# The down projection of a decoder layer: running sums in PSUM banks, weight differences on VectorE, chunks of eight pairs

## The chip, the cores and the metric

The kernel runs on one core of a Trainium2 chip. A core has a matrix engine (TensorE, in the profile PE; PEld is its weight load), VectorE (DVE), ScalarE (ACT), GpSimd (POOL) and SyncE (SP), which issues most of the DMAs. TensorE's products land in eight banks of PSUM, everything else works in SBUF. The metric is the device time of one execution in microseconds; before the change three runs took 1473.42, 1476.03 and 1476.26 us, a median of 1476.03 us.

## The reference

One decoder layer over 1024 tokens of width 1024. The part that the change touches is the second half of the MLP with its residual, and the final norm, in float32:

```
def squared_relu_mlp(xn, w_ff1, w_ff2):
    hdn = jnp.square(jax.nn.relu(xn @ w_ff1))      # [1024, 4096]
    return hdn @ w_ff2                             # the down projection, [1024, 1024]

h = h + mixer_block(...)
h = h + squared_relu_mlp(rmsnorm(h, norm_mlp_gain[l]), w_ff1[l], w_ff2[l])
return rmsnorm(h, norm_final_gain)
```

## The kernel before, in words

The large products are made in 2 x 2 blocks with seven block products instead of eight (Strassen's algorithm in Winograd's form). For the down projection the blocks are halves of the tokens (rows), of a pair of hidden tiles (contraction) and of the width (columns). With `b11`, `b12`, `b21`, `b22` the blocks of a weight pair, and `a11`, `a12`, `a22` and the sums `s1` to `s4` the hidden side, which the up projection has left in DRAM (`hid_d`), the products are P1 = a11 b11, P2 = a12 b21, P3 = s4 b22, P4 = a22 T4, P5 = s1 T1, P6 = s2 T2 and P7 = s3 T3, with T1 = b12 - b11, T2 = b22 - T1, T3 = b22 - b12 and T4 = b21 - T2. With U2 = P1 + P6 and U3 = U2 + P7, the blocks of the result are P1 + P2, U2 + P5 + P3, U3 + P4 and U3 + P5, each on top of the residual (`h2_d`).

Float32 accuracy is reached by splitting: `split_unit` makes of a [128, 512] operand a high part (ScalarE, L110, `da` and `db` on the hidden and on the weight side) and a low part (VectorE, L111: operand minus high part). Each product of two operands is three matmuls: high-high, high-low, low-high. A unit (one pair of hidden tiles in one of the seven products) takes 12 matmuls: three for each of four token tiles, which sit in four PSUM banks.

Before, the 16 pairs of hidden tiles go in four chunks of `NQ` = 4. A chunk runs its seven products one after the other, four units each: 28 products of 48 matmuls, 1344 in all. The units are split four ahead of their use (`wpool` has five buffers for each of its two tags). After each product `collect` empties its four banks into a sum of its own in SBUF (`accp...`, eight places of four tiles; four of them begin as the residual): VectorE adds (L267), or in the first chunk ScalarE copies (L1236). The banks are then free for another product, which begins afresh. The weight differences T1 to T4 are made by GpSimd (`sums`, L1205), into `temps` (`down_temp`) or in place. In the last chunk, whose order is P1, P2, P5, P6, P3, P7, P4, the sums over the products are made as well: GpSimd's `late_sums` after P6 (twelve additions, L267 on POOL), additions on VectorE, and the final norm of each row of tokens: `row_share` (a square sum on ScalarE, L1216, and a multiplication by the gain on GpSimd, L1218) and `row_end` (square sum L1222, square root L1223, reciprocal L1225, two scalings L1226 and L1227, and the stores).

What sets the order: the program is traced in the order of the code, and a scheduler puts each engine's instructions into a fixed list; each engine and the SyncE queue then work through their lists in order, waiting on semaphores. SBUF for the large operands is eight slots of 2 MB (`slot`), which the weights (`y...`), the hidden operands (`x...`) and the sums (`accp...`) take as they come free. `first_loads` starts the loads while the last group of the up projection runs, and all of them are issued by SyncE.

Of the kernel before, what the change touches and what calls it, by code (L numbers as in the profile page):

```python
# [22 lines left out]
NT = SEQ // P          # token tiles  # L23
KT = D // P            # contraction tiles over the model width
# [4 lines left out]
NM = DFF // P          # hidden tiles  # L29
LATE = 6               # token tiles from here on get the second norm's factors on ScalarE  # L30
EARLY = 4              # pairs of hidden tiles whose first products fill the gap of the second norm
NQ = 4                 # pairs of hidden tiles per chunk of the down projection
NORM_EPS = 1e-6        # of the group norm too
NEG_INF = -1e30

# tiles of 128 x 1024 in the weight stream
# [51 lines left out]
def block_kernel(ctx, tc, x, xT, wbig, cols, rows, ctab, amask, amask_u, out):  # L88
# [28 lines left out]
    def gmm(ps, lhsT, rhs, start, stop):  # L117
        """A large product; pieces of the background follow it."""
        pe.matmul(ps, lhsT=lhsT, rhs=rhs, start=start, stop=stop)  # L119
        bg.tick(ps.shape[-1] / 2.4)  # L120

# [46 lines left out]
    causal = const.tile([P, P], F32, name="causal")      # [key, query]: key <= query  # L168
# [32 lines left out]
    units = [0]  # L201

    def split_unit(name, src):
        """A [128, 512] operand in its two parts."""
# [5 lines left out]
    def w_raw(bl, g):  # L210
        """b11, b21, b12, b22 of a pair of tiles with the weights stationary."""
# [38 lines left out]
    def four(slot_, i):  # L250
        """Half i of a slot: four tiles of [128, 512]."""
# [941 lines left out]
    with tc.tile_pool(name="p6", bufs=1) as p6:  # L1193
# [37 lines left out]
        def collect(c, n, banks, tts):  # L1231
            """The banks of a product into its sum; in the last chunk also the sums over the products."""
            for tt in tts:
# [8 lines left out]
                if c < nchunk - 1:  # L1242
                    continue
# [158 lines left out]
```

## Time and profile before

| | |
|---|---|
| median of three runs | 1476.03 us (1473.42 to 1476.26) |
| span of the profiled execution, first to last instruction | 1472.3 us |
| time of the profiled execution beyond its span | not on the page; the median run is 3.7 us above the span |
| TensorE busy | 1415.5 us, 96% of the span |
| VectorE busy | 1200.1 us, 82% |
| ScalarE busy | 754.0 us, 51% |
| GpSimd busy | 441.7 us, 30% |
| granted TensorE clock, mean | 0.987 |
| down projection, first to last matmul | 1147.3 to 1465.1 us |

Busy shares are averages over the whole span. What a change of the down projection is worth has to be read from its own stretch, the last 325 us: where TensorE is idle there, what it waits for, and how fast its matmuls follow each other. Records of one line can be those of a helper (L110, L111, L119 and L267 are), so the names of the tiles tell which product they belong to: `dp` are the banks of the down projection, `da` and `db` its split operands, `u66p` the banks of the up projection.

### The profile page before, as it was taken

The page shows a single profiled execution, that of the slowest core. Times are in us where ns is not written, and L with a number is a line of the kernel's source. Part 1 is how long each engine was busy: PE and PEld are TensorE (multiplying, and loading weights), DVE is VectorE, ACT ScalarE, POOL GpSimd, SP SyncE. Part 2 cuts the span into 40 slices and gives each one's busy share as a digit, 9 for nine tenths or more (in the row PEclk, how much of TensorE's full clock was granted, in tenths as well). Part 3 has the DMA queues.
Part 4 walks back from the last instruction along what each step waited for, and adds up shares of the span by engine and source line. Part 5 has one row for each costly group of instructions (what it writes and reads, how often), then busy time and mean ns, then how long its engine had stood idle before and what let it go on. Part 6 is the DMA issues. An engine that isn't in the chain of part 4 may idle for free.

```text
span 1472.3 us, 19724 instructions
## 1 busy us (share of the span) xinstructions
PE 1415.5 (96%) x6656; PEld 1164.7 (79%) x6656; DVE 1200.1 (82%) x2043; ACT 754.0 (51%) x1553; POOL 441.7 (30%) x278
## 2 busy tenths in 40 slices
PE   6999999999999999899997989999999999999996
PEld 5888788878788888777885768888888878888884
DVE  7557888898777877999899998866666689788997
ACT  6544676666453444542154754655555554444444
POOL 3005121310000000574065174322220444135465
PEclk9999999999999999999999999999999999999997
DMA  5534334343320213028340336544446944453413
GB/s 203 176 109 132 131 102 126 102 131 116 121 58 29 86 44 143 16 86 323 121 171 29 115 108 209 206 157 150 157 144 209 365 155 143 144 172 129 157 58 114
DMA packets 93363, 200.57 MB, mean 136 GB/s; under 512 B 9808, under 2 KB 19792, under 8 KB 93008
## 3 DMA queue, kind: packets, MB, share of 16 engines
q1 hardware_dynamic: 73728, 176.23, 35.3%
q10 hardware_dynamic: 19536, 23.10, 4.4%
q8 instruction: 52, 0.85, 0.2%
q14 instruction: 47, 0.39, 0.1%
HBM read 142.14 MB, written 57.15 MB: 135 GB/s over the span
## 4 chain that ended last, share of the span: by engine, by line
PE 67%; DVE 15%; POOL 2%; issue 2%; DMA 1%; ACT 1%; SPq 0%; ACTq 0%; DVEq 0%; POOLq 0%
PE u66p L119 17%; PE dp L119 17%; PE u8p L119 11%; PE r L119 11%; PE ya L119 3%; PE ro L710 1%; POOL accp L267 1%; DVE res L267 1%; PE pv L620 1%; PE pss L578 1%; DVE xp_s L942 1%; DVE accp L267 1%; PE yrp L119 1%; DVE da L111 1%; DVE db L111 1%
## 5 line engine op out<-in xcount | busy, mean ns | idle before, releaser
L119 PE MATMUL dp<-db,da 128*128 128x512 f32 x1344 | 309.5, 392 | 8.3 <-DVE db L111 8.1
L119 PEld LDWEIGHTS dp<-db,da 128*128 128x128 f32 x1344 | 253.3, 189 | 64.4 <-DVE db L111 10.9
L119 PE MATMUL r<-wh,x 128*128 128x512 f32 x512 | 167.0, 395 | 0.0
L110 ACT ACTIVATE da<-x 128x512 fp32r<-128x512 f32 x112 | 70.8, 632 | 142.6 <-PE dp L119 136.9
L119 PE MATMUL u66p<-xp_s,w66t 128*128 128x512 f32 x576 | 134.2, 390 | 3.4 <-ACT w66t L110 3.0
L119 PEld LDWEIGHTS u66p<-xp_s,w66t 128*128 128x128 f32 x576 | 108.0, 188 | 26.6 <-ACT w66t L110 3.4
L111 DVE TENSOR_TENSOR da<-x,da 128x512 fp32r<-128x512 f32 x112 | 100.9, 901 | 31.8 <-ACT da L110 31.7
L119 PEld LDWEIGHTS r<-wh,x 128*128 128x128 f32 x512 | 94.0, 188 | 16.1 <-issue 0.8
L119 PE MATMUL r<-wl,x 128*128 128x512 f32 x256 | 101.3, 396 | 0.0
L322 POOL TENSOR_TENSOR rup<-rup 128x512 f32<-128x512 f32 x4 | 11.5, 2908 | 288.6 <-DVE yr_p L322 288.6
L119 PE MATMUL u8p<-xs,w8t 128*128 128x512 f32 x396 | 94.3, 392 | 0.0
L119 PE MATMUL u66p<-xp_a,w66b 128*128 128x512 f32 x384 | 92.1, 396 | 0.0
L119 PEld LDWEIGHTS u8p<-xs,w8t 128*128 128x128 f32 x396 | 73.6, 188 | 15.7 <-issue 0.8
L119 PEld LDWEIGHTS u66p<-xp_a,w66b 128*128 128x128 f32 x384 | 72.9, 191 | 15.1
L111 DVE TENSOR_TENSOR db<-y,db 128x512 fp32r<-128x512 f32 x80 | 72.3, 904 | 6.2 <-ACT db L110 6.1
L232 POOL TENSOR_TENSOR up_room<-pair 128x512 f32<-128x512 f32 x16 | 26.5, 1656 | 133.8 <-DVE w66t L111 120.1
L1035 ACT ACTIVATE ha<-ha 128x512 f32<-128x512 f32 x64 | 40.4, 632 | 46.7 <-DVE ha L1034 42.5
L119 PE MATMUL u8p<-x,w8b 128*128 128x512 f32 x264 | 64.1, 393 | 0.0
L111 DVE TENSOR_TENSOR w66t<-up_room,w66t 128x512 fp32r<-128x512 f32 x60 | 50.4, 848 | 9.6 <-ACT w66t L110 9.3
L267 DVE TENSOR_TENSOR accp<-dp,accp 128x512 f32<-128x512 f32 x92 | 57.4, 680 | 1.0 <-PE dp L119 1.0
L119 PEld LDWEIGHTS u8p<-x,w8b 128*128 128x128 f32 x264 | 48.9, 188 | 10.6 <-issue 0.8
L110 ACT ACTIVATE w66t<-up_room 128x512 fp32r<-128x512 f32 x60 | 36.9, 626 | 36.9 <-PE u66p L119 24.5
(543 smaller groups left out, 3367.1 us busy)
## 6 DMA issues: line engine op xcount, KB each, us to landing
pair<-in_wbig_dram SPq DMA_DIRECT2D x62, 512.0 KB, 3.7
x<-hid_d SPq DMA_DIRECT2D x112, 256.0 KB, 5.1
hid_d<-ha SPq DMA_DIRECT2D x61, 256.0 KB, 2.1
raw<-in_wbig_dram SPq DMA_DIRECT2D x26, 512.0 KB, 4.1
y<-in_wbig_dram SPq DMA_DIRECT2D x24, 512.0 KB, 6.1
hid_d<-s SPq DMA_DIRECT2D x45, 256.0 KB, 2.9
gate_d<-go ACTq DMA_DIRECT2D x44, 256.0 KB, 2.1
gate<-gate_d SPq DMA_DIRECT2D x32, 256.0 KB, 4.6
```

The costliest lines, as they stand in the source:

```text
L110: act_e.activation(h, src, AF.Copy)
L111: dve.tensor_tensor(l, src, h.bitcast(F32), op=ALU.subtract)
L119: pe.matmul(ps, lhsT=lhsT, rhs=rhs, start=start, stop=stop)
L232: pool_e.tensor_tensor(t3, b22, b12, op=ALU.subtract)
L267: e.tensor_tensor(dst, a, b, op=ALU.add)
L322: e.tensor_tensor(o[q], x[q], y[q], op=op)
L578: pe.matmul(pss[:, j * 256:j * 256 + nk * P], lhsT=qT[:, hd * P:(hd + 1) * P], rhs=kT[:, hd // AG, s, 0:nk, :], start=(s == 0), stop=(s == 1))
L620: pe.matmul(o, lhsT=vv[:, tv, g * ADH:(g + 1) * ADH], rhs=p_.rearrange("p (j u) n -> p j u n", u=2)[:, 2 * g:2 * g + 2, u, :], start=p_ is ...
L710: pe.matmul(o, lhsT=a, rhs=b, start=start and n == 0, stop=stop and n == 2)
L942: dve.tensor_tensor(l, src, h.bitcast(F32), op=ALU.subtract)
L1035: act_e.activation(o, o, AF.Relu)
```

## The change

Chunks are eight pairs (`NQ` = 8): two chunks of seven products of 96 matmuls, the same 1344 matmuls. Every chunk has the order P2, P1, P5, P6, P3, P7, P4, and only three of the seven begin afresh in their banks. P6, P7 and P4 run on in the banks of P1, so these hold P1, U2, U3 and U3 + P4 in turn, and P3 runs on in the banks of P5. After each product `collect` makes one addition per token tile on VectorE, into one of four result blocks (`res_acc`, tiles `acc0`, `acc1`) that begin as the residual. The separate sums, `late_sums` and ScalarE's copies are gone. T1 to T4 are made on VectorE, in the places of blocks that are done with (`made`, `place`), and `row_share`'s multiplication by the gain is on VectorE too, so GpSimd has no instruction left in this stage. Each weight block is loaded by itself, in transfers of 256 KB (a half of a tile's columns) where before the first chunk alone did that and the others took whole tiles of 512 KB. Each product's hidden operand has a slot of its own. P7 runs its last two units bank by bank, since P4 goes on in the same banks, and the last product its last four.

```diff
-NQ = 4                 # pairs of hidden tiles per chunk of the down projection
+NQ = 8
...
-    def gmm(ps, lhsT, rhs, start, stop):
+    def gmm(ps, lhsT, rhs, start, stop, more=False):
...
-        pe.matmul(ps, lhsT=lhsT, rhs=rhs, start=start, stop=stop)
+        pe.matmul(ps, lhsT=lhsT, rhs=rhs, start=start, stop=stop, skip_group_check=more)
...
-    seq = [(c, n) for c in range(nchunk - 1) for n in ("p1", "p2", "p5", "p7", "p6", "p4", "p3")]
-    seq += [(nchunk - 1, n) for n in ("p1", "p2", "p5", "p6", "p3", "p7", "p4")]
+    order = ("p2", "p1", "p5", "p6", "p3", "p7", "p4")
+    seq = [(c, n) for c in range(nchunk) for n in order]
...
     def first_loads():
         load_hidden(0)
-        load_weight_blocks(0, 0, 0)
+        load_weight_block(0, "b21")
         load_hidden(1)
-        load_weight_blocks(0, 1, 0)
-        load_weight_blocks(0, 0, 1)
-        load_weight_blocks(0, 1, 1)
-        load_hidden(2)
-        load_hidden(3)
...
+        load_weight_block(0, "b11")
+        load_residual()
+        load_weight_block(0, "b12")
+        load_weight_block(0, "b22")
...
-        def sums(c, *names):
...
-                    pool_e.tensor_tensor(o, a, b, op=ALU.subtract)
...
+        place = {"p2": "b21", "p1": "b11", "p5": "b11", "p6": "b11", "p3": "b22", "p7": "b12", "p4": "b21"}
+        made = {"p5": ("b11", "b12", "b11"), "p6": ("b11", "b22", "b11"), "p3": ("b21", "b21", "b11"),
+                "p7": ("b12", "b22", "b12")}
+
+        def weight_sum(u):
...
+            (c, n), q = seq[u // NQ], u % NQ
+            if n in made:
+                o, a, b = (wblocks[c, m][:, q] for m in made[n])
+                dve.tensor_tensor(o, a, b, op=ALU.subtract)
...
-            pool_e.tensor_tensor(block, block, gfin[:, j * 512:(j + 1) * 512], op=ALU.mult)
+            dve.tensor_tensor(block, block, gfin[:, j * 512:(j + 1) * 512], op=ALU.mult)
...
-        def late_sums(tt):
-            p4, p5, p6_, h22 = (acc[k][:, tt] for k in ("p4", "p5", "p6", "h22"))
-            add_to(p5, p5, p6_, pool_e)
-            add_to(h22, h22, p5, pool_e)
-            add_to(p4, p4, p6_, pool_e)
...
+        into = {"p2": (0, 0), "p1": (0, 0), "p5": (1, 1), "p6": (0, 1), "p3": (0, 1), "p7": (1, 1), "p4": (1, 0)}
+
+        def collect(c, n, tt):
+            i, j = into[n]
+            dst = res_acc[i, j][:, tt]
+            add_to(dst, banks[n][tt], dst)
...
+            if n == "p1":
+                row_share(tt, dst, 0)
+            elif n == "p3":
+                row_end(tt, res_acc[0, 0][:, tt], dst, 1)
+            elif n == "p7":
+                row_share(4 + tt, dst, 1)
+            elif n == "p4":
+                row_end(4 + tt, res_acc[1, 1][:, tt], dst, 0)
+
+        ahead = 4
...
+            if n in ("p2", "p5"):
+                banks[n] = [ax_bank(f"d{n}_{c}_{tt}") for tt in range(4)]
+            elif n == "p3":
+                banks[n] = banks["p5"]
+            elif n == "p1":
+                banks[n] = banks["p6"] = banks["p7"] = banks["p4"] = [mm_bank(f"dp1_{c}_{tt}") for tt in range(4)]
+            fresh = n in ("p1", "p2", "p5")
...
+            tail = 4 if last else 2 if n == "p7" else 0
+            for q in range(NQ):
+                u = i * NQ + q
+                weight_sum(u + ahead + 1)
+                operands(u + ahead)
...
+                if q == NQ - ahead:
+                    load_hidden(i + 2)
```

Where this puts the instructions shows in the engines' lists. First SyncE's list as the down projection begins; `x0` to `x6` are hidden operands of the products in turn, `y0_...` weights of the first chunk, `accp...` and `acc...` the places of the sums, and the rows are those of before, then those of now.

```order
L1111 DMA y0_1_10814<-in_wbig_dram 128x512 x4
L1123 DMA x2_10827<-hid_d_7346 128x512 x8
L1127 DMA accp2_10836<-h2_d_7345 128x512 x8
L1127 DMA accp3_10837<-h2_d_7345 128x512 x8
L1123 DMA x4_11063<-hid_d_7346 128x512 x8
L1123 DMA x6_11248<-hid_d_7346 128x512 x8
```

```order
L1120 DMA x1_10818<-hid_d_7346 128x512 x8
L1110 DMA y0_b11_10827<-in_wbig_dram 128x512 x8
L1128 DMA acc0_10836<-h2_d_7345 128x512 x8
L1128 DMA acc1_10845<-h2_d_7345 128x512 x8
L1110 DMA y0_b12_10854<-in_wbig_dram 128x512 x8
L1110 DMA y0_b22_10863<-in_wbig_dram 128x512 x8
L1120 DMA x2_11092<-hid_d_7346 128x512 x8
```

In both programs 32 transfers stand ahead of the residual's 16, of which the last 12 and the last 16 are shown. Before, the hidden operands of the first four products were among them, and those of the fifth to the eighth followed the residual. Now the operands of the first two products are among them, and the third's (`x2`, for P5) stands behind the residual and the 16 transfers of `b12` and `b22`.

Then VectorE in the first chunk, now, from the emptying of P2's banks (`dp2`) on; `da12`, `db12` and so on are the operands of P1's last four units, `da16`, `db16` those of P5's first.

```order
L267 TENSOR_TENSOR acc0_10836<-dp2_0_3_11001,acc0_10836 128x512
L111 TENSOR_TENSOR da12_11163<-x1_10818,da12_11163 128x512
L111 TENSOR_TENSOR db12_11166<-y0_b11_10827,db12_11166 128x512
L1203 TENSOR_TENSOR y0_b11_10827<-y0_b12_10854,y0_b11_10827 128x512
L111 TENSOR_TENSOR da13_11181<-x1_10818,da13_11181 128x512
L111 TENSOR_TENSOR db13_11184<-y0_b11_10827,db13_11184 128x512
L1203 TENSOR_TENSOR y0_b11_10827<-y0_b12_10854,y0_b11_10827 128x512 x3
L111 TENSOR_TENSOR da14_11199<-x1_10818,da14_11199 128x512
```

The weight differences (L1203) stand between the splits. Between the emptying of P2's banks and that of P1's, 16 of the chunk's 32 stand there, and 36 VectorE instructions in all (4 additions, 16 splits, 16 differences); between P1's and P5's again 36; after that no difference is left in the chunk, and a product has about 20 instructions. In the second chunk the corresponding stretches have 26, 36 and 38, four of the last on 128 x 1 operands.

Last, VectorE just before the last product, P4: before, with `accp3` the block that P3 completes and `da27` P4's operands; then now, with `acc1` the block that P7 is added to, `dp1_1_...` the shared banks and `da107` P4's fourth unit.

```order
L267 TENSOR_TENSOR accp3_10837<-accp3_10837,accp1_10838 128x512 x2
L267 TENSOR_TENSOR accp3_10837<-dp3_3_2_13232,accp3_10837 128x512
L267 TENSOR_TENSOR accp3_10837<-dp3_3_3_13233,accp3_10837 128x512
L1225 RECIPROCAL rn3_10957<-rn3_10957 128x1 x2
L267 TENSOR_TENSOR accp3_10837<-accp3_10837,accp1_10838 128x512
L1227 SCALAR_TENSOR_TENSOR accp3_10837<-accp3_10837,rn3_10957,gfin_10956 128x512 x2
L267 TENSOR_TENSOR accp3_10837<-accp3_10837,accp1_10838 128x512
L111 TENSOR_TENSOR da27_0_13350<-x26_13013,da27_0_13350 128x512
```

```order
L267 TENSOR_TENSOR acc1_10845<-dp1_1_2_12341,acc1_10845 128x512
L1218 TENSOR_SCALAR rn3_10973<-rn3_10973 128x1
L1219 TENSOR_TENSOR acc1_10845<-acc1_10845,gfin_10972 128x512
L111 TENSOR_TENSOR da107_13169<-x13_12950,da107_13169 128x512
L111 TENSOR_TENSOR db107_13172<-y1_b21_11763,db107_13172 128x512
L1218 TENSOR_SCALAR rn3_10973<-rn3_10973 128x1
L1219 TENSOR_TENSOR acc1_10845<-acc1_10845,gfin_10972 128x512
L267 TENSOR_TENSOR acc1_10845<-dp1_1_3_12342,acc1_10845 128x512
```

Before, the first operand of P4 stands behind additions of `accp1`, which GpSimd's `late_sums` has to finish first. Now the first three operands of P4 stand ahead of all this, and what stands late is the emptying of P7's fourth bank: behind the split of P4's fourth unit and two multiplications by the gain. P4's matmuls of its first unit for that fourth bank wait for it; TensorE's list has 12 of P4's matmuls ahead of them.

## Rows read from the trace of the kernel before

**Rows 1.** The page: the span, then busy us (share of the span) xinstructions of each engine.

```profile
span 1472.3 us, 19724 instructions
...
PE 1415.5 (96%) x6656; PEld 1164.7 (79%) x6656; DVE 1200.1 (82%) x2043; ACT 754.0 (51%) x1553; POOL 441.7 (30%) x278
```

**Rows 2.** Who TensorE waited for, 1140 to 1473 us: total, times, longest.

```profile
PE dp L119 <- DVE db L111: 8.1, 5, 6.5
PE dp L119 <- ACT db L110: 0.2, 1, 0.2
```

**Rows 3.** Timeline of TensorE in the down projection: start, us, xcount, [idle before <-releaser].

```profile
1147.29 33.12 PE L119 MATMUL dp<-db,da 128*128 128x512 f32 x145
...
1187.54 255.97 PE L119 MATMUL dp<-db,da 128*128 128x512 f32 x1128 [0.38 <-DVE db L111]
1450.05 1.65 PE L119 MATMUL dp<-db,da 128*128 128x512 f32 x3 [6.54 <-DVE db L111]
...
1454.02 11.07 PE L119 MATMUL dp<-db,da 128*128 128x512 f32 x41 [0.20 <-ACT db L110]
```

**Rows 4.** Busy time by stretch: engines, then granted clock (PEclk), DMA share, GB/s.

```profile
1420.00:1430.00 10.00, 10.00 (x46) 8.28 (x45) 10.00 (x18) 3.74 (x7) 5.20 (x2) 1.00 0.01 2
...
1440.00:1450.00 10.00, 3.51 (x16) 2.58 (x14) 9.09 (x7) 3.69 (x10) 8.84 (x6) 0.84 0.28 105
1450.00:1460.00 10.00, 9.27 (x26) 6.24 (x27) 9.96 (x21) 6.06 (x13) 4.30 (x3) 0.65 0.28 105
```

**Rows 5.** Timeline of GpSimd (POOL), end of the down projection.

```profile
1410.16 4.94 POOL L1218 TENSOR_TENSOR accp<-accp,gfin 128x512 f32<-128x512 f32 x3 [1.39 <-ACT junk L1216]
1424.80 24.05 POOL L267 TENSOR_TENSOR accp<-accp,accp 128x512 f32<-128x512 f32 x12 [9.70 <-DVE accp L267]
```

**Rows 6.** Timeline of VectorE (DVE), end of the down projection.

```profile
1412.15 1.78 DVE L111 TENSOR_TENSOR db<-down_temp,db 128x512 fp32r<-128x512 f32 x1
...
1418.56 0.68 DVE L111 TENSOR_TENSOR db<-y,db 128x512 fp32r<-128x512 f32 x1
1419.16 0.68 DVE L111 TENSOR_TENSOR da<-x,da 128x512 fp32r<-128x512 f32 x1
...
1440.91 1.77 DVE L267 TENSOR_TENSOR accp<-accp,accp 128x512 f32<-128x512 f32 x1 [1.12 <-POOL accp L267]
...
1447.64 1.75 DVE L111 TENSOR_TENSOR da<-x,da 128x512 fp32r<-128x512 f32 x1
```

**Rows 7.** Groups by line and shape, 1147 to 1473 us: xcount | busy us, mean ns.

```profile
L111 DVE TENSOR_TENSOR da<-x,da 128x512 fp32r<-128x512 f32 x107 | 97.5, 911 | 31.8 <-ACT da L110 31.7
...
L267 DVE TENSOR_TENSOR accp<-dp,accp 128x512 f32<-128x512 f32 x92 | 57.4, 680 | 1.0 <-PE dp L119 1.0
...
L267 POOL TENSOR_TENSOR accp<-accp,accp 128x512 f32<-128x512 f32 x20 | 37.2, 1896 | 9.7 <-DVE accp L267 9.7
L1205 POOL TENSOR_TENSOR y<-y,y 128x512 f32<-128x512 f32 x16 | 26.2, 1665 | 55.7 <-DMA y<-in_wbig_dram 55.7
```

**Rows 8.** Timeline of VectorE at the start of the down projection: sums of two SBUF tensors.

```profile
1147.55 0.69 DVE L1168 TENSOR_TENSOR s<-s,ha 128x512 f32<-128x512 f32 x1
1148.16 0.69 DVE L1170 TENSOR_TENSOR ha<-ha,ha 128x512 f32<-128x512 f32 x1
```

**Rows 9.** Timeline of SyncE's queue (SPq): first loads of the down projection.

```profile
1144.19 8.40 SPq L1123 DMA_DIRECT2D x<-hid_d  x8
1152.99 12.29 SPq L1127 DMA_DIRECT2D accp<-h_d  x16
```

**Rows 10.** DMA issues, 1130 to 1200 us: xcount, KB each, median us to landing.

```profile
accp<-h_d SPq DMA_DIRECT2D x16, 256.0 KB, 5.9
```

**Rows 11.** Timeline of all engines after the last matmul.

```profile
1465.13 0.69 DVE L267 TENSOR_TENSOR accp<-dp,accp 128x512 f32<-128x512 f32 x1
...
1466.04 0.61 ACT L1222 ACTIVATE junk<-accp 128x512 f32<-128x512 f32 x1
...
1467.83 0.72 ACT L1226 ACTIVATE accp<-accp,rn 128x512 f32<-128x512 f32 x1 [0.29 <-DVE rn L1225]
```

More of the change, by code (lines that the diff above doesn't have):

```diff
@@ L1129, in first_loads, with load_residual @@
+    def load_residual():
+        for i in range(2):
+            two = slot(f"acc{i}", F32).rearrange("p (j t n) -> p j t n", j=2, t=4)
+            for j in range(2):
+                res_acc[i, j] = two[:, j]
+                for n in range(4):
+                    nc.sync.dma_start(two[:, j, n], h2_d[4 * i + n][:, j * 512:(j + 1) * 512])
     def first_loads():
         load_hidden(0)
-        load_weight_blocks(0, 0, 0)
+        load_weight_block(0, "b21")
         load_hidden(1)
-        load_weight_blocks(0, 1, 0)
@@ L1260, in late_sums @@
-        def late_sums(tt):
-            p4, p5, p6_, h22 = (acc[k][:, tt] for k in ("p4", "p5", "p6", "h22"))
-            add_to(p5, p5, p6_, pool_e)
-            add_to(h22, h22, p5, pool_e)
-            add_to(p4, p4, p6_, pool_e)
-        ops = [operands(0, q) for q in range(NQ)]
-        for i, (c, n) in enumerate(seq):
-            after = i + 1 < len(seq)
-            if n == "p2":
-                sums(c, *(("t1", "t3") if c < nchunk - 1 else ("t1",)))
-            if n == "p5":
-                sums(c, "t2")
-                if c == nchunk - 1:
-                    sums(c, "t3")
-                sums(c, "t4")
-            banks = [(ax_bank, mm_bank)[i % 2](f"d{n}_{c}_{tt}") for tt in range(4)]
-            nxt = []
-            def part(q, tt):
-                a, b = ops[q]
-                for k, (x, y) in enumerate(((0, 0), (0, 1), (1, 0))):
-                    gmm(banks[tt], a[:, x, tt * P:(tt + 1) * P], b[:, y, :], q == 0 and k == 0,
-                        q == NQ - 1 and k == 2)
-            if not after:
+        into = {"p2": (0, 0), "p1": (0, 0), "p5": (1, 1), "p6": (0, 1), "p3": (0, 1), "p7": (1, 1), "p4": (1, 0)}
@@ new lines, in block_kernel, with part @@
+        ahead = 4
+        banks = {}
+        for u in range(ahead):
+            operands(u)
+        for i, (c, n) in enumerate(seq):
+            if n in ("p2", "p5"):
[5 more added lines that the diff above has]
+            fresh = n in ("p1", "p2", "p5")
+            last = i + 1 == len(seq)
+            def part(u, tt):
+                a, b = ops[u]
+                q = u % NQ
+                for k, (x, y) in enumerate(((0, 0), (0, 1), (1, 0))):
+                    gmm(banks[n][tt], a[:, x, tt * P:(tt + 1) * P], b[:, y, :], fresh and q == 0 and k == 0,
+                        q == NQ - 1 and k == 2, not fresh)
+            tail = 4 if last else 2 if n == "p7" else 0
[3 more added lines that the diff above has]
+                operands(u + ahead)
+                if q < NQ - tail:
+                    for tt in range(4):
+                        part(u, tt)
+                if q == NQ - ahead:
+                    load_hidden(i + 2)
+                    if c + 1 < nchunk and n in ("p3", "p7"):
+                        load_weight_block(c + 1, {"p3": "b21", "p7": "b11"}[n])
+            for tt in range(4):
+                for q in range(NQ - tail, NQ):
+                    part(i * NQ + q, tt)
+                if tail:
+                    collect(c, n, tt)
+            if not tail:
@@ L1286, in block_kernel @@
                 for tt in range(4):
-                    for q in range(NQ):
-                        part(q, tt)
-                    collect(c, n, banks, (tt,))
-                continue
+                    collect(c, n, tt)
             for q in range(NQ):
-                nxt.append(operands(i + 1, q))
-                for tt in range(4):
-                    part(q, tt)
-            collect(c, n, banks, range(4))
-            ops = nxt
-            if i % 2 == 0:
-                load_hidden(i + 4)
-                load_hidden(i + 5)
@@ L1300, in block_kernel @@
-            if c == nchunk - 1:
-                if n == "p6":
-                    for tt in range(4):
-                        late_sums(tt)
-                elif n == "p1":
-                    nc.sync.dma_start(gfin, rows[:, D:2 * D])
-            elif n == "p5":
-                load_weight_blocks(c + 1, 0)
-            elif n == "p4":
-                load_weight_blocks(c + 1, 1)
+                del ops[i * NQ + q]
+            if n == "p4" and c + 1 < nchunk:
+                for m in ("b12", "b22"):
+                    load_weight_block(c + 1, m)
@@ L1312, in _tables @@
+            if c + 1 == nchunk and n == "p2":
+                nc.sync.dma_start(gfin, rows[:, D:2 * D])
 def _tables():
```

77 lines of the change are left out of this document (18 added, 59 removed).

## The prediction, made before the changed kernel ran

> **What bounds the kernel now.** I read the page first: TensorE is busy for 1415.5 of 1472.3 us [rows 1], so a change of the down projection is worth what TensorE stands still or runs slowly there, and nothing that another engine saves counts by itself. The waits of TensorE in this stage come next: 8.1 us on VectorE's low parts in five waits and 0.2 us on ScalarE, the longest 6.5 us [rows 2]. TensorE's timeline puts them in place [rows 3]: the first `dp` matmul starts at 1147.29, the wait of 6.54 us ends at 1450.05, and the last matmul ends at 1454.02 + 11.07 = 1465.09. The 1128 matmuls of the long run follow each other every 255.97 / 1128 = 0.2269 us. Then the clock by stretch [rows 4]: full until the wait, 0.84 and 0.65 on average in the 20 us around and after it, which is a mix of the two levels, 2.4 and 1.2 GHz. The last 47 matmuls show the price: from 1450.05 to 1465.09 less the two waits inside (0.7) is 14.4 us, where 47 x 0.2269 = 10.7 would do.
>
> Who makes the long wait is read from the two other timelines. GpSimd's twelve `late_sums` occupy it from 1424.80 for 24.05 us [rows 5]; VectorE's addition at 1440.91 waits for one of them, and P4's first operand is split only at 1447.64, behind it in VectorE's list [rows 6]. Beside GpSimd's work a VectorE instruction on two SBUF operands often takes 1.75 to 1.78 us; in the stretch in which GpSimd is silent (1415.1 to 1424.8) the same instruction starts every 0.60 us (1418.56, 1419.16) [rows 5, 6].
>
> **The change part by part.** The matmuls stay: 28 x 48 = 14 x 96 = 1344. At the steady pace they take 1344 x 0.2269 = 305.0 us. If nothing holds TensorE, the last one ends at 1147.3 + 305.0 = 1452.3 instead of 1465.1: a gain of 12.8 us. Its parts are the waits (8.3), the slow clock after the long one (3.7) and 0.8 us lost around the three short waits before 1187.5.
>
> *Sums.* Away go the eight sums in SBUF, with 92 additions out of PSUM before (0.68 us each), 20 additions on GpSimd (1.90 us) and 16 copies on ScalarE [rows 7]; in come 14 x 4 = 56 additions of the first kind. All this lay beside TensorE's work except `late_sums`. So the removal is worth the wait before P4 and the slow clock, counted above, if nothing takes their place.
>
> *Weight differences.* 64 instructions of GpSimd (four groups of 16 like the one of 1.67 us [rows 7]) become 64 of VectorE. The rows have such an operation on VectorE, with two SBUF inputs and a float32 result: starts 0.61 us apart [rows 8]. They are bunched: 36 VectorE instructions stand between two emptyings of banks in the densest stretches, two in the first chunk, one and a nearly equal one (38, four of them tiny) in the second. 36 x 0.605 = 21.8 us, and a product is 96 x 0.2269 = 21.8 us. VectorE just keeps up there, and in the other products 20 x 0.605 = 12.1 us leave it room. Operands are split four units ahead, 4 x 12 x 0.2269 = 10.9 us, so a lag of a few us reaches nobody. I take 0. The bounds: if no cover is left, the lag by the mean duration before, 0.911 us [rows 7], which is the third rival; and no gain, since TensorE's waits are already counted as gone. The three short waits go, because they lay where VectorE shared the time with GpSimd's first differences.
>
> *Loads.* Up to the residual SyncE's list has the same 48 transfers, so the start of the stage stays at 1147.3. The residual's 16 are issued from 1152.99 to 1165.28, 0.77 us each [rows 9]. By that rate `b12` is issued from 1165.3 on, `b22` from 1171.5 on, and `x2` from 1177.6 on; with 5.9 us to landing [rows 10] the first piece of `x2` is there at 1183.5. P5 begins at 1147.3 + 2 x 21.8 = 1190.9. ScalarE wants `x2` from 1180.0 on, four units earlier, and waits some 3.5 us for it; the split then needs about 2 us (estimated: two instructions on each of ScalarE and VectorE). 5.4 us are left, so the cost is 0; the bound is the slower rate of the eight transfers before, 8.40 / 8 = 1.05 us [rows 9], in the first rival. `b12` is wanted at 1171.7 at the earliest, when VectorE has emptied P2's banks, and lands at about 1171.2. The second chunk's blocks follow one product or more ahead of their use, and SyncE's list is thinner there: 0.
>
> The Trainium skill has a rule against this part: in "DMA: Bandwidth & Descriptors", section Bandwidth, transfers should be batched to 1 MiB, with 341 GB/s at 1 MB and 138 GB/s at 64 KB; halving the 512 KB weight transfers goes the other way. If 256 KB fell in the middle, at some 240 GB/s (an estimate from that page), a transfer would take 1.1 us, about the first rival's rate. The trace does not bear it out: 16 transfers of 256 KB in flight together took 12.29 us, 341 GB/s.
>
> *Banks.* The emptying of a bank is a new wait for TensorE in one place of each chunk, since P4 goes on in P7's banks. Three of the four banks are ready early, as P7's last two units run bank by bank. The fourth, in the last chunk, is emptied behind a split and two multiplications in VectorE's list: about 2.6 us after P7's end (estimated: the split's two high parts and a square on ScalarE at 0.6 each, then two VectorE instructions at 0.6 to 0.7). TensorE has 12 matmuls, 2.7 us, to do first. I take 0; the bounds are 0 and 2.7 us late at two places. P6, P3 and the fresh products have a whole product between.
>
> *Norm.* The multiplications by the gain move from GpSimd to VectorE, 8 x 0.6 us in stretches with room. After P3 in the last chunk ScalarE has four rows to end before it can split P7's fifth unit; in series a row takes 1466.04 to 1468.55, 2.5 us [rows 11], so at most 10.0 us, under the 10.9 of the look-ahead. Cost 0.
>
> *End.* From the last matmul to the end of the span it is 1472.3 - 1465.1 = 7.2 us, the same instructions as now. The last tile's square started 0.2 us after its addition had ended, as ScalarE was still at the tile before [rows 11]; without the backlog up to 0.7 us may go (estimated). I keep 7.2.
>
> **Sum.** Span 1452.3 + 7.2 = 1459.5 us, 12.8 below 1472.3. The profiled execution's own time is not on the page; the median run is 3.7 us above its span, and what lies around the span does not change. 1459.5 + 3.7 gives 1463 us.
>
> **The rivals.** First, the early loads are late. For it: the DMA engines are full there, and ten transfers of slack is not much. At 1.05 us each, `x2` is issued at 1153.0 + 32 x 1.05 = 1186.6, lands at 1192.5 and is split by 1194.5: TensorE waits 3.6 us at P5. A wait may bring the slow clock as in [rows 4], up to 3.7 us: 1467 to 1470 us. Against it: the rate of 0.77 us held for the 16 transfers just before.
>
> Second, TensorE's waits come back at the end in another form: at the fourth bank of P7, or behind ScalarE and VectorE waiting for each other in the norm. Price: 2.7 us at each of two banks, and up to 3.7 for the clock: 1466 to 1472 us; only if the look-ahead were used up several times over would nothing be left (1473 to 1479).
>
> Third, slower: VectorE becomes the bound in the dense stretches. Its slow instructions would then come from something other than GpSimd, and the mean of 0.911 us would stay. A dense product takes 36 x 0.911 = 32.8 us, 11.0 more than TensorE; two in a row are 22.0, less the look-ahead of 10.9 is 11.1 us per chunk and 22 us in all: 1485 us. It decides against the change from a spacing of 0.85 us on, where (72 x 0.85 - 43.6 - 10.9) x 2 eats the 12.8. Against it stand the rows with 0.60, one group of them from the first 50 us of this stage with its full DMA load [rows 6, 8].
>
> **How the numbers follow.** TensorE runs through, 1460 to 1466 us: 0.78. Late loads: 0.09. Waits at the end: 0.06. Hardly anything left: 0.02. VectorE as the bound: 0.05. A difference below 0.2%, 3 us, can't be told from none: faster 0.93, same 0.02, slower 0.05. The likeliest case gives 1463 us. Runs of one kernel lie up to 3 us apart and the end may be 0.7 us shorter, so the range begins at 1459; it ends at 1470, which takes in the first two rivals but for their worst.
>
> **What would show it.** Right: TensorE has one unbroken run of 1344 matmuls over 305 us with the clock at 1.00 until it ends; VectorE's splits last 0.68 us throughout; GpSimd has no row after 1147 us; the last matmul ends near 1452. Wrong: a TensorE wait near 1191 on a split of `x2` (first rival), near the last P4 or P7 (second), or one that grows through P1 and P5 with VectorE busy without a break (third); or a matmul spacing other than 0.227 us in running sums, which no row of before could show.

## The result, and the profile after

| | before | changed |
|---|---|---|
| median | 1475.31 us (4 runs, 1473.42 to 1476.26) | 1463.15 us (4 runs, 1461.25 to 1463.77) |
| ratio to before | | 0.9919, 95% interval 0.9902 to 0.9936 |
| span of the profiled execution | 1472.3 us | 1461.9 us |
| first `dp` matmul to the last one's end | 317.8 us | 305.4 us |
| from there to the end of the span | 7.2 us | 6.8 us |

The changed kernel is 12.2 us faster; 1463 was forecast, in 1459 to 1470. The timeline of TensorE after (start, us, xcount) answers to [rows 3]:

```profile
1149.74 305.38 PE L119 MATMUL dp<-db,da 128*128 128x512 f32 x1344
```

1344 matmuls without a break, 305.38 us; TensorE waits for nobody in the stage. The windows (busy us of PE, PEld, DVE, ACT, POOL, then granted clock, DMA share, GB/s) answer to [rows 4]:

```profile
1170.00:1190.00 20.00, 20.00 (x90) 16.57 (x89) 20.00 (x34) 8.38 (x15) 0.00 (x0) 1.00 1.05 387
1190.00:1210.00 20.00, 20.00 (x90) 16.57 (x89) 20.00 (x34) 8.23 (x15) 0.00 (x0) 1.00 0.44 149
...
1430.00:1440.00 10.00, 10.00 (x44) 7.97 (x43) 9.03 (x19) 7.24 (x16) 0.00 (x0) 1.00 0.00 0
1440.00:1450.00 10.00, 10.00 (x46) 8.28 (x45) 3.93 (x8) 2.94 (x7) 0.00 (x0) 1.00 0.00 0
```

The clock is at 1.00 up to the end, GpSimd has no row, and VectorE is busy for 20.00 of 20 us in the two dense stretches: it is as full there as it can be, and TensorE never waits for it.

The stage begins at 1149.7 here and at 1147.3 before. In the eleven other profiled executions of this study it begins between 1146.3 and 1151.9, with no clear relation to the edits. So kernels are compared below by the length of the stage and of the end behind it, and by the medians.

### The profile page after: what moved, and what is told of

Read it like the earlier page. It is cut to its first block, busy times and chain, and to the rows that moved or that the text cites. A ratio compares the mean times of both kernels' runs of the same rounds, so it can differ in the third digit from the quotient of the medians.

```text
span 1461.9 us, 19529 instructions
## 1 busy us (share of the span) xinstructions
PE 1415.8 (97%) x6656; PEld 1166.7 (80%) x6656; DVE 1145.2 (78%) x2059; ACT 746.6 (51%) x1537; POOL 288.8 (20%) x186
## 4 chain that ended last, share of the span: by engine, by line
PE 70%; DVE 12%; POOL 2%; DMA 2%; issue 1%; ACT 1%; SPq 0%; ACTq 0%; DVEq 0%; POOLq 0%
PE dp L119 20%; PE u66p L119 16%; PE u8p L119 11%; PE r L119 11%; PE ya L119 3%; PE ro L710 1%; DVE res L267 1%; PE pv L620 1%; PE pss L578 1%; PE yrp L119 1%; PE op L119 1%; PE rs L710 1%; POOL out L322 1%; DMA res<-in_x_dram 1%; DVE xp_s L942 1%
## 5 line engine op out<-in xcount | busy, mean ns | idle before, releaser
L119 PE MATMUL dp<-db,da 128*128 128x512 f32 x1344 | 305.4, 389 | 0.0
L111 DVE TENSOR_TENSOR da<-x,da 128x512 fp32r<-128x512 f32 x112 | 77.3, 690 | 69.2 <-ACT da L110 69.0
L119 PEld LDWEIGHTS r<-wh,x 128*128 128x128 f32 x512 | 94.0, 188 | 16.1 <-issue 0.8
L111 DVE TENSOR_TENSOR db<-y_b,db 128x512 fp32r<-128x512 f32 x112 | 76.7, 685 | 4.7 <-ACT db L110 4.7
L110 ACT ACTIVATE db<-y_b 128x512 fp32r<-128x512 f32 x112 | 69.1, 617 | 9.0 <-DMA y_b<-in_wbig_dram 5.2
L119 PE MATMUL u66p<-xp_a,w66t 128*128 128x512 f32 x192 | 50.5, 414 | 4.4 <-DVE xp_a L942 2.8
L119 PEld LDWEIGHTS r<-wl,x 128*128 128x128 f32 x256 | 48.2, 188 | 8.2 <-issue 0.4
```

The source lines that it names most:

```text
L110: act_e.activation(h, src, AF.Copy)
L111: dve.tensor_tensor(l, src, h.bitcast(F32), op=ALU.subtract)
L119: pe.matmul(ps, lhsT=lhsT, rhs=rhs, start=start, stop=stop, skip_group_check=more)
```

## The experiments

The theory was that the gain is TensorE's waits and the slow clock behind the long one, all of which go when no one on TensorE's path waits for GpSimd. The main rival was that it is in the running sums and the larger chunks. "Stage" is the first `dp` matmul to the last one's end, "waits" TensorE's own in it, "end" what follows up to the end of the span, each from one profiled execution. The kernel before ran beside them each time, with medians of 1475.2 to 1476.1 us; the ratios are to those runs.

| kernel | median us | ratio to before, 95% | stage | waits | end |
|---|---|---|---|---|---|
| before | 1475.3 | | 317.8 | 8.3 | 7.2 |
| late_on_vector | 1472.9 | 0.9974 to 0.9998 | 310.9 | 3.7 | 11.0 |
| diff_on_vector | 1471.9 | 0.9969 to 0.9990 | 315.0 | 5.1 | 7.2 |
| both_on_vector | 1468.3 | 0.9938 to 0.9967 | 306.9 | 1.4 | 11.0 |
| changed | 1463.2 | 0.9902 to 0.9936 | 305.4 | 0 | 6.8 |
| changed_small_chunks | 1464.2 | 0.9912 to 0.9936 | 305.6 | 0 | 7.0 |
| changed_no_running_sums | 1464.4 | 0.9914 to 0.9938 | 305.8 | 0.4 | 6.7 |
| changed_no_running_small | 1488.2 | 1.0069 to 1.0103 | 326.3 | 11.6 | 12.5 |
| changed_diff_on_gpsimd | 1472.9 | 0.9959 to 0.9987 | 315.0 | 5.4 | 6.8 |
| changed_gpsimd_noise | 1479.5 | 1.0009 to 1.0029 | 321.5 | 9.1 | 6.8 |
| changed_more_vector | 1463.9 | 0.9897 to 0.9926 | 305.4 | 0 | 6.7 |
| changed_half_transfers | 1467.8 | 0.9924 to 0.9951 | 311.0 | 3.4 | 6.7 |

### One part at a time, in the kernel before

**late_on_vector**

```diff
-            add_to(p5, p5, p6_, pool_e)
-            add_to(h22, h22, p5, pool_e)
-            add_to(p4, p4, p6_, pool_e)
+            add_to(p5, p5, p6_)
+            add_to(h22, h22, p5)
+            add_to(p4, p4, p6_)
```

> The kernel before with one edit: the twelve additions of late_sums are on VectorE instead of GpSimd. My theory: the long wait before P4 (6.5 us) and the slow clock behind it (3.7 us) come from GpSimd's 24 us for these additions. On VectorE they take 12 x 0.605 = 7.3 us, right behind the emptying of P6's banks (1421.7 plus about 3.4, so until about 1432.4). The first operand of P7 now stands behind them in VectorE's list and is ready at 1433.7, where TensorE wants it at 1432.6: a new wait of about 1 us, and one of about 0.5 us before P4. So some 1.5 us of waits stay of 7.2 and the clock stays full: 9 us less than before, 1466 us (1464 to 1469). Rival: VectorE's own list, 16 to 28 instructions per product of 10.9 us, is what makes P4 late, whoever makes the sums: the wait before P4 stays above 4 us and the time within 3 us of before, 1473 to 1477.

The time fell by some 2 us, not 9. TensorE's timeline:

```profile
1434.72 12.57 PE L119 MATMUL dp<-db,da 128*128 128x512 f32 x48 [2.83 <-DVE db L111]
1447.70 10.30 PE L119 MATMUL dp<-db,da 128*128 128x512 f32 x44 [0.41 <-DVE db L111]
```

The wait of 6.54 us before P4 is down to 0.41, so GpSimd's additions did make it; a wait of 2.83 us before P7 is new, larger than the 1 us that was expected. The stage is 6.9 us shorter. The rest of the miss is behind the last matmul, which ends at 1458.0: from VectorE's and ScalarE's timeline there,

```profile
1452.62 1.88 DVE L267 TENSOR_TENSOR accp<-accp,dp 128x512 f32<-128x512 f32 x3
...
1456.99 0.68 DVE L267 TENSOR_TENSOR accp<-accp,dp 128x512 f32<-128x512 f32 x1
...
1457.59 0.69 DVE L267 TENSOR_TENSOR accp<-dp,accp 128x512 f32<-128x512 f32 x1
...
1459.53 0.69 DVE L267 TENSOR_TENSOR accp<-dp,accp 128x512 f32<-128x512 f32 x1
...
1465.23 0.35 ACTq L1229 DMA_DIRECT2D out_dram<-accp  x1
```

VectorE is still adding P7 into two blocks (`accp<-accp,dp`, eight additions) until 1457.6. P4's first bank is emptied only then, and the last at 1459.53; the four rows of the norm follow one after another on ScalarE, and the last store is issued at 1465.23, 7.2 us after the last matmul. In the kernel before it is 3.5 us (1468.58), in the changed kernel 2.8 us (1457.92). In the kernel before the same eight additions lay beside the slow clock: they ended at 1460.15, while TensorE was at P4 until 1465.09, and VectorE then waited for TensorE:

```profile
1452.70 1.88 DVE L267 TENSOR_TENSOR accp<-accp,dp 128x512 f32<-128x512 f32 x3
...
1459.47 0.68 DVE L267 TENSOR_TENSOR accp<-accp,dp 128x512 f32<-128x512 f32 x1
...
1462.41 0.69 DVE L267 TENSOR_TENSOR accp<-dp,accp 128x512 f32<-128x512 f32 x1 [0.99 <-PE dp L119]
```

The theory was right on the wait before P4 and wrong on the time: over half of what the stage gave (3.8 of 6.9 us) was taken back at the end. The rival had the time about right (within 3 us of before) and the reason wrong, since the wait before P4 did not stay above 4 us. The edit also gives VectorE twelve additions more (7.3 us), and no run tells how much of the new wait and of the longer end is theirs.

**diff_on_vector**

```diff
-                    pool_e.tensor_tensor(o, a, b, op=ALU.subtract)
+                    dve.tensor_tensor(o, a, b, op=ALU.subtract)
```

> The kernel before with one edit: the 64 weight differences T1 to T4 are on VectorE instead of GpSimd; late_sums stay on GpSimd. My theory: this part is worth the three short waits before 1187.5 (1.0 us) and the 0.8 us lost around them, and the long wait before P4 stays: 1473.5 us (1472 to 1475.5), a ratio of 0.998 to 1.000. Rival: what the change gains comes from a VectorE that GpSimd no longer slows (911 ns falls to 690 ns for the splits), so that most of the 12 us appears with this edit alone: 1464 to 1468. A third: 64 more instructions make VectorE late and the time grows by several us.

```profile
1151.94 294.65 PE L119 MATMUL dp<-db,da 128*128 128x512 f32 x1297
1451.03 1.65 PE L119 MATMUL dp<-db,da 128*128 128x512 f32 x3 [4.44 <-DVE db L111]
```

The short waits are gone, in one run of 1297 matmuls, and the long wait is still there, 4.44 us instead of 6.54. The medians give 3.3 us, the ratio's interval 1.5 to 4.6 us, the stage 2.8: a little more than the 1.8 that this part had in the sum, and far from the rival's whole gain. What is more in the stage is the shorter long wait (2.1), less the slow clock behind it: the last 47 matmuls take 15.3 us without their waits, and took 14.4 before.

**both_on_vector**: the two diffs together.

> The kernel before with both edits: late_sums and the weight differences on VectorE; chunks of four pairs, the eight separate sums and the banks are as before. My theory: what counts is that nothing on TensorE's path waits for GpSimd, and the gains of the two edits add up: about 10.5 us, 1465 us (1463 to 1468), of which 1 to 1.5 us of waits before P7 and P4 are left against the changed kernel. Rival: running the sums on in PSUM and the larger chunks have a gain of their own (fewer additions, fewer banks to empty), and this kernel stays 5 us or more above the changed one: 1468 or more.

```profile
1431.34 11.17 PE L119 MATMUL dp<-db,da 128*128 128x512 f32 x48 [1.01 <-DVE db L111]
1442.92 10.28 PE L119 MATMUL dp<-db,da 128*128 128x512 f32 x44 [0.41 <-DVE db L111]
```

Only 1.0 us before P7 and 0.4 before P4 are left, and the stage is within 1.5 us of the changed kernel's. But the end is again 11.0 us. 1.5 + 4.2 = 5.7 us, which is about the 5.1 between the medians. So the rival was right that something more is in the change; the next three runs test two candidates for it.

### Running sums and the size of the chunks

**changed_small_chunks**: `NQ = 4` in the changed kernel, blocks and operands in half of a slot each.

> The changed kernel with chunks of four pairs (NQ = 4) instead of eight: 28 products of 48 matmuls, 112 additions out of the banks instead of 56. My theory: the size of the chunks is worth nothing by itself, since VectorE has 12 to 18 instructions per product of 10.9 us (7.3 to 10.9 us): 1463 us, at most 1467 where the bank of P7 or the loads of b12 and b22, which are issued only after the P4 of the chunk before, come a little late in one of the four chunks. Rival: the larger chunks give the loads and the emptying the time they need; without them TensorE waits 2 to 3 us in each chunk and the time is 1471 to 1476.

**changed_no_running_sums**

```diff
-        into = {"p2": (0, 0), "p1": (0, 0), "p5": (1, 1), "p6": (0, 1), "p3": (0, 1), "p7": (1, 1), "p4": (1, 0)}
+        into = {"p2": ((0, 0),), "p1": ((0, 1), (1, 1), (1, 0), (0, 0)), "p5": ((0, 1), (1, 1)),
+                "p6": ((0, 1), (1, 1), (1, 0)), "p3": ((0, 1),), "p7": ((1, 0), (1, 1)), "p4": ((1, 0),)}
...
+            banks[n] = [(ax_bank, mm_bank)[i % 2](f"d{n}_{c}_{tt}") for tt in range(4)]
+            fresh = True
```

> The changed kernel with the running sums undone and all else kept (chunks of eight, differences on VectorE): each of the seven products begins afresh in four banks, in turn the one half of PSUM and the other, and is added out of its banks into every result block that it belongs to, 14 additions per token tile and chunk instead of 7: 112 instead of 56. The experiments with late_sums and both edits left 4 us at the end (11.0 us from the last matmul to the end instead of 7), because VectorE still had P7's eight additions to make while the short last product ran. My theory: that end belongs to products of 48 matmuls; with 96 the last product lasts 21.8 us and VectorE has 28 instructions (17 us) beside it. In the densest stretch there are 75 instructions in two products, 45.4 us against 43.6, a lag that the look-ahead covers. So no wait, an end of 7 us, 1463 to 1465 us. Rival: fewer additions are worth the 5 us between the kernel with both edits and the changed one, at any chunk size: 1467 or more, with an end near 11 us.

**changed_no_running_small**: that diff and `NQ = 4`.

> The changed kernel with both the running sums undone and chunks of four pairs: 28 products of 48 matmuls, 224 additions out of the banks. My theory: running sums and larger chunks can stand in for each other, and only without either does the time grow. VectorE has 128 instructions per chunk, 77 us, against 76 us of matmuls: after P1 it is 7 us behind, after P6 about 11, which is the look-ahead, so TensorE waits 0 to 3 us in a chunk, and the last product of 10.9 us is too short for P7's eight additions: an end of 10 to 11 us. 1467 to 1475 us, I take 1470. Rival: the differences being on VectorE is all that counts and the additions fit in between: 1463 to 1465, an end of 7 us.

The four kernels make a square: 1463.2 with both, 1464.2 with small chunks, 1464.4 without running sums, 1488.2 with neither. TensorE's timeline of the last one, where the pattern of the first lines comes back in all four chunks:

```profile
1185.54 0.50 PE L119 MATMUL dp<-db,da 128*128 128x512 f32 x1 [1.19 <-DVE acc L267]
1186.74 11.21 PE L119 MATMUL dp<-db,da 128*128 128x512 f32 x48 [0.70 <-DVE db L111]
...
1210.74 0.51 PE L119 MATMUL dp<-db,da 128*128 128x512 f32 x1 [1.29 <-DVE acc L267]
1212.55 77.63 PE L119 MATMUL dp<-db,da 128*128 128x512 f32 x335 [1.30 <-DVE db L111]
```

TensorE waits for splits and for banks that VectorE has not emptied (`DVE acc`). VectorE is busy for 50.00 of 50 us there, with 224 additions out of the banks in the whole stage:

```profile
1250.00:1300.00 50.00, 48.47 (x213) 39.56 (x212) 50.00 (x85) 20.21 (x35) 0.00 (x0) 1.00 0.33 108
```

It was expected at 1470; the count (77 us of VectorE per 76 us of matmuls) was right, but the lag does not stay under the look-ahead, and the banks, emptied late, hold up TensorE as well. So leaving out one of the two parts costs 1 us, which is within the scatter of the runs, and leaving out both costs 25. Each part halves VectorE's additions out of the banks (56 with both, 112 with one, 224 with neither), and one halving is needed. All four kernels have the new order of the products, the loads of single blocks and the norm's multiplication on VectorE; what these are worth by themselves no run shows. In the changed kernel no gap of TensorE is left in the stage, and no run points to a version beyond it.

### VectorE and GpSimd side by side

**changed_diff_on_gpsimd**

```diff
-                dve.tensor_tensor(o, a, b, op=ALU.subtract)
+                pool_e.tensor_tensor(o, a, b, op=ALU.subtract)
```

> The changed kernel with one edit: the 64 weight differences are on GpSimd again. My theory: GpSimd takes 1.67 us for each, 16 in a row 26.7 us, and while it works the splits on VectorE take 1.77 us instead of 0.69. VectorE has only 20 instructions per product of 21.8 us left, so it falls behind by about as much as the look-ahead of 10.9 us covers: waits of 0 to 4 us in all, 1463 to 1469 us, and VectorE's splits near 0.9 us on average. Rival: differences on GpSimd are as good (VectorE has fewer instructions), no wait at all and 1461 to 1464. A third: the waits are as large as the whole gain, 1473 or more.

```profile
L1203 POOL TENSOR_TENSOR y_b<-y_b,y_b 128x512 f32<-128x512 f32 x64 | 110.5, 1748 | 169.4 <-DVE db L111 96.1 <-DMA y_b<-in_wbig_dram 68.3 <-DVE rn L1218 3.1
L111 DVE TENSOR_TENSOR db<-y_b,db 128x512 fp32r<-128x512 f32 x108 | 105.5, 977 | 3.5 <-ACT db L110 3.5
```

```profile
1203.99 3.01 PE L119 MATMUL dp<-db,da 128*128 128x512 f32 x12 [0.37 <-DVE db L111]
1207.39 3.01 PE L119 MATMUL dp<-db,da 128*128 128x512 f32 x12 [0.39 <-DVE db L111]
...
1363.93 99.78 PE L119 MATMUL dp<-db,da 128*128 128x512 f32 x431 [2.58 <-DVE db L111]
```

In the groups (xcount | busy, mean ns) the splits of the weights take 977 ns where they take 685 in the changed kernel, and TensorE gets its units late. The stage is 9.6 us longer, 5.4 of it waits; the forecast of up to 6 was too small, and the time is at the third alternative's edge (1473). In the kernel before, the same part gave 2.8.

**changed_gpsimd_noise**

```diff
+        for _ in range(24):
+            pool_e.tensor_tensor(extra, res_acc[1, 0][:, 0], res_acc[1, 0][:, 1], op=ALU.subtract)
```

> The changed kernel with 24 subtractions added on GpSimd, of two SBUF tensors into a tile that nobody reads, from about 1168 us on, beside the dense stretches of VectorE in the first chunk. Nothing waits for them. My theory, the third rival of the prediction made to happen: VectorE's instructions with two SBUF operands take 1.77 us while GpSimd works (24 x 1.67 = 40 us); 32 of 36 in a dense product are such, so in 40 us VectorE ends about 24 instructions where it needs 66. It falls 25 us behind, the look-ahead covers 10.9, TensorE waits about 10 to 15 us around P5 and loses up to 3.7 us more by the clock: 1473 to 1482 us. Rival: instructions of VectorE are slow for another reason (the kind of operand, the DMA traffic), GpSimd's work changes nothing: 1463.

VectorE's groups while GpSimd works:

```profile
L1204 DVE TENSOR_TENSOR y_b<-y_b,y_b 128x512 f32<-128x512 f32 x10 | 17.5, 1788 | 0.0
L111 DVE TENSOR_TENSOR db<-y_b,db 128x512 fp32r<-128x512 f32 x6 | 10.7, 1780 | 0.0
...
L267 DVE TENSOR_TENSOR acc<-dp,acc 128x512 f32<-128x512 f32 x4 | 2.5, 676 | 0.0
```

```profile
1189.42 4.62 PE L119 MATMUL dp<-db,da 128*128 128x512 f32 x12 [3.49 <-DVE db L111]
1196.22 4.61 PE L119 MATMUL dp<-db,da 128*128 128x512 f32 x12 [2.19 <-DVE db L111]
1203.04 0.50 PE L119 MATMUL dp<-db,da 128*128 128x512 f32 x1 [2.21 <-DVE db L111]
1204.73 264.16 PE L119 MATMUL dp<-db,da 128*128 128x512 f32 x1150 [1.19 <-DVE da L111]
```

Instructions with two SBUF operands take 1.78 us, those with one operand in PSUM 0.68 as ever. The DMA traffic is not the cause: its share is 1.01 from 1165 to 1185 and 0.38 in the 20 us after that, with most splits at 1.7 to 1.8 us in both, and 1.05 in the changed kernel with splits of 0.69. The stage grows by 16.1 us, of which 9.1 are waits (10 to 15 were expected) and the rest the clock (0.79 and 0.86 in the 40 us from 1185). This is the prediction's third rival, and here it took GpSimd to bring it about. The Trainium skill says the same ("SBUF — State Buffer", section Who interferes with whom): VectorE's second pair of SBUF ports is shared with GpSimd under an exclusive lock, and a VectorE instruction with at most one SBUF input stays out of it; the 0.68 us with a PSUM operand agree.

It is not always VectorE that loses. In the kernel before, one of the twelve `late_sums` took 7.26 us (the other eleven 1.5 on average), while eight splits on VectorE beside it took 0.69 us each:

```profile
1426.37 7.26 POOL L267 TENSOR_TENSOR accp<-accp,accp 128x512 f32<-128x512 f32 x1
```

```profile
1427.57 0.69 DVE L111 TENSOR_TENSOR da<-x,da 128x512 fp32r<-128x512 f32 x1
...
1431.78 0.69 DVE L111 TENSOR_TENSOR db<-y,db 128x512 fp32r<-128x512 f32 x1
```

GpSimd's addition ended at 1433.63, 1.2 us after the last of these splits; in diff_on_vector one took 6.05 us and ended 1.2 us after such a row too. So a part of the 24.05 us that the prediction read as GpSimd's work was very likely GpSimd held up by VectorE; no run tests that by itself.

**changed_more_vector**

```diff
+                if n in made:
+                    dve.tensor_tensor(extra, a, b, op=ALU.subtract)
```

> The changed kernel with every weight difference made twice on VectorE, the second time into a tile that nobody reads: 64 instructions more, 38.7 us of VectorE time. The list then has 36 of VectorE's instructions per product in four products of the first chunk instead of two. My theory: 36 x 0.605 = 21.8 us is just a product's time, so four in a row are as good as two: TensorE does not wait, 1463 us (1461 to 1466). Rival: there is no room at 36 per product, and a lag that two products hide under the look-ahead comes out after four: 1467 or more.

```profile
1149.15 305.42 PE L119 MATMUL dp<-db,da 128*128 128x512 f32 x1344
```

64 more instructions, no wait: in the first chunk the stretch of 36 per product just lasts for four products instead of two, 21.8 us each.

### The early loads

**changed_half_transfers**

```diff
+            for k in range(0, 512, 256):
+                nc.sync.dma_start(t[:, q, k:k + 256], hid_d[part, c * NQ + q][:, k:k + 256])
```

and the same for the weights.

> The changed kernel with every 256 KB load of the down projection's weights and hidden operands cut into two of 128 KB (half the columns). My theory: with all queues full the rate is set by the DMA engines, not by the size of one transfer, as 16 transfers of 256 KB moved at 341 GB/s in the trace of before; 128 KB transfers go at much the same rate, or a tenth below, the first piece of P5's hidden operand is still there before 1190, and the time stays at 1463 us (1461 to 1466). The Trainium skill (DMA: Bandwidth & Descriptors, section Bandwidth) gives 138 GB/s at 64 KB and 341 GB/s at 1 MB; 128 KB would lie at some 190 GB/s (an estimate from that page). Rival by that rule: a pair of halves takes 1.4 us instead of 0.69, the piece of x2 that P5 begins with arrives 20 us later or more, TensorE waits at P1 and P5 and the time is 1480 us or more.

SyncE's queue of this kernel, then of the changed one, from the loads of `b12` and `b22` on:

```profile
1175.18 16.42 SPq L1111 DMA_DIRECT2D y_b<-in_wbig_dram  x32
1191.69 20.48 SPq L1122 DMA_DIRECT2D x<-hid_d  x39
```

```profile
1166.57 10.96 SPq L1110 DMA_DIRECT2D y_b<-in_wbig_dram  x16
1177.94 10.44 SPq L1120 DMA_DIRECT2D x<-hid_d  x16
```

```profile
1196.33 0.73 PE L119 MATMUL dp<-db,da 128*128 128x512 f32 x2 [2.50 <-ACT da L110]
1197.97 263.09 PE L119 MATMUL dp<-db,da 128*128 128x512 f32 x1150 [0.91 <-DVE da L111]
```

A transfer of 128 KB takes 16.42 / 32 = 0.513 us, 255 GB/s; one of 256 KB takes 10.96 / 16 = 0.685 us, 383 GB/s. `x2` is issued 13.8 us later, and TensorE waits 3.4 us at P5: the first rival of the prediction made to happen, at the price that it named (3.6). Both expectations failed, 1463 and 1480.

What set the rate is seen in the last two columns of the windows (DMA share, GB/s), of this kernel and then of the changed one:

```profile
1180.00:1190.00 10.00, 10.00 (x46) 8.29 (x45) 9.12 (x15) 3.05 (x5) 0.00 (x0) 1.00 0.88 278
```

```profile
1180.00:1190.00 10.00, 10.00 (x46) 8.29 (x45) 10.00 (x18) 4.65 (x8) 0.00 (x0) 1.00 1.05 387
```

In the changed kernel SyncE's queue waits for earlier transfers during some 5 of the 11 us of the 16 issues from 1166.57, and a transfer lands 5.4 us after its issue. With the halves it waits 0.3 us in the 11 us from 1180, the DMA engines are no longer full, and a transfer lands after 3.2 us. So at 128 KB SyncE's issuing, one transfer every 0.51 us, is the limit, and not the DMA engines; the theory that the engines set the rate failed there. What the engines could do with such transfers from a faster source no run shows. So the rule of the Trainium skill ("DMA: Bandwidth & Descriptors", section Bandwidth), whose figures are for transfers issued by GpSimd, is not tested by this run: the 255 GB/s are already above the 190 estimated from its figures, and at 256 KB the 383 GB/s are above the 341 that it gives for 1 MB.

## Why the prediction was right

**Steps that came out.** The stage: 305.0 us forecast, 305.4 measured, at the same spacing in running sums as in fresh banks. Stage and end together are 12.8 us shorter (325.0 less 312.2), the forecast's gain; the end is 6.8 instead of 7.2. Loads: `x2` was forecast to be issued from 1177.6 and used at 1183.5; it was issued at 1177.94 (that it came so close is partly luck: `b12` was issued 1.3 us later than forecast, and the 16 transfers took 0.685 us each instead of 0.77), and ScalarE's timeline has its first split at 1183.32:

```profile
1183.32 0.63 ACT L110 ACTIVATE da<-x 128x512 fp32r<-128x512 f32 x1
```

P5 begins at 1149.7 + 43.6 = 1193.3, so with VectorE's half of the split, which ends at 1184.9, 8.4 us are left; 5.4 were forecast, and 2.4 of the difference is the later start of the stage. Dense stretches: VectorE's timeline, from the emptying of P2's banks to that of P1's,

```profile
1170.93 2.48 DVE L267 TENSOR_TENSOR acc<-dp,acc 128x512 f32<-128x512 f32 x4
...
1192.72 2.48 DVE L267 TENSOR_TENSOR acc<-dp,acc 128x512 f32<-128x512 f32 x4
```

1192.72 - 1170.93 = 21.8 us for 36 instructions, as worked out. Banks: P7 of the last chunk ends at about 1149.74 + 13 x 21.8 = 1433.3, and its fourth bank is emptied

```profile
1434.44 0.68 DVE L1219 TENSOR_TENSOR acc<-acc,gfin 128x512 f32<-128x512 f32 x1
...
1435.04 0.69 DVE L267 TENSOR_TENSOR acc<-dp,acc 128x512 f32<-128x512 f32 x1
...
1435.78 4.18 PEld L119 LDWEIGHTS dp<-db,da 128*128 128x128 f32 x19 [0.40 <-DVE acc L267]
```

at 1435.73, 2.4 us later (2.6 forecast), behind the multiplication by the gain. The next weight load waited 0.40 us for it, and the 12 matmuls ahead of it (2.7 us) just covered that.

**Two small errors that cancelled.** The 3.7 us between span and median compared two different executions; in each of the four runs of the changed kernel time and span are 1.9 us apart, in those of the kernel before that ran beside the experiments 2.1 to 2.2. And the stage began 2.4 us later than in the profiled execution of before. 1459.5 + 2.4 = 1461.9 is the span measured, and with 1.9 it is 1463.8, the time of that execution. Either error alone would have moved the forecast by 2 us.

**The step that was wrong, though the total was right.** "All this lay beside TensorE's work except `late_sums`. So the removal is worth the wait before P4 and the slow clock, counted above, if nothing takes their place." Something did take their place when `late_sums` went to VectorE. The list of the sums in the prediction leaves out VectorE's own in the kernel before, beside the 92:

```profile
L267 DVE TENSOR_TENSOR accp<-accp,accp 128x512 f32<-128x512 f32 x12 | 12.2, 1043 | 3.6 <-POOL accp L267 3.6
...
L267 DVE TENSOR_TENSOR accp<-accp,dp 128x512 f32<-128x512 f32 x8 | 5.1, 684 | 0.0
```

These 20 additions, 17.3 us, were priced at nothing; the eight lay beside the slow clock behind the wait. In late_on_vector, where the twelve moved ones are in VectorE's list as well, the end is 3.8 us longer and 2.83 us of wait stand before P7; in both_on_vector it is 3.8 and 1.01. The whole change leaves VectorE 56 additions instead of 112 and gives a product twice the time, so the sum held.

In the same way the weight differences had 1.8 us in the sum, gave 2.8 alone in the kernel before, and cost 9.6 when they were put back on GpSimd in the changed kernel. So a part has no price of its own: what counts is whether VectorE keeps up in each product, and several parts each buy that.

The third rival was given 0.05 on the ground that its slow instructions would need another source than GpSimd; that was the right ground. The forecast that VectorE just keeps up (21.8 us of work in 21.8) held as well: it is full in two products of each chunk, changed_more_vector shows that a longer stretch of the same instructions does no harm, and changed_gpsimd_noise that slower ones do at once.

## What to carry to other kernels

Price an edit that takes a wait away by the work that was hidden under the wait, not by the wait: list what the neighbouring engines still have to do at that place and at the end of the program, and what the moved work adds to it. When an engine off the path is near full, edits that relieve it replace each other; test them in a square (each alone, both, neither) before crediting one. Compare profiled executions by the length of the changed stage, since here its start alone differed by up to 5.6 us between executions.

## What was not expected of the hardware

The price of a wait differed with its length. After the waits of 1.01 and 0.41 us in both_on_vector the granted clock is 1.00 in every window of 10 us; after waits of 2.5 to 2.8 us (three kernels) such windows show 0.83 to 0.92, and after the 4.44 us in diff_on_vector

```profile
1450.00:1460.00 10.00, 8.30 (x18) 5.35 (x19) 9.96 (x21) 5.90 (x13) 3.32 (x2) 0.50 0.29 106
```

0.50, which is the lower level, for 10 us. But the length of one wait does not settle it: in changed_no_running_small two waits of 1.3 us each, which ended 1.8 us apart, left

```profile
1450.00:1460.00 10.00, 8.46 (x24) 6.53 (x25) 9.11 (x16) 3.84 (x7) 0.00 (x0) 0.66 0.00 1
```

0.66, and a like pair 0.83 in the window from 1210. With the clock at 1.00, each short wait of 0.4 us in changed_diff_on_gpsimd still lengthened a unit of 12 matmuls from 2.72 to 3.40 us, more than the wait itself. And a transfer of 128 KB is small enough that SyncE, issuing one every 0.51 us, held the rate a third below that of 256 KB.
